# Stick-breaking attention: sums over later key blocks made on VectorE, one product with minus ones per key block

## The chip, the cores and the metric

The kernel runs on one core of one Trainium2 chip. The core has a matrix engine (TensorE, PE in the rows below), a vector engine (VectorE, DVE), a scalar engine (ScalarE, ACT), GpSimd (POOL) and SyncE (SP); GpSimd and SyncE do little here but issue DMAs. The metric is the device time of one execution in microseconds (us), as the median of several.

## The reference, cut to what matters

One layer of an encoder: 512 prompt frames and 32 sample frames go through one input projection, a retention branch of 4 heads, a stick-breaking branch of 8 heads, gates, an output projection and an MLP. The change is in the stick-breaking branch of the prompt.

```python
def stick_breaking_block(q, k, v, q_pos, k_pos):
    z = jnp.einsum('bqhd,bkhd->bhqk', q, k).astype(jnp.float32) * (SB_HEAD_DIM ** -0.5)
    mask = (k_pos[None, :] < q_pos[:, None])[None, None]
    u = jnp.where(mask, jax.nn.log_sigmoid(-z), 0.0)
    after = lax.cumsum(u, axis=3, reverse=True) - u
    w = jnp.where(mask, jnp.exp(jax.nn.log_sigmoid(z) + after), 0.0)
    return jnp.einsum('bhqk,bkhd->bqhd', w.astype(v.dtype), v)
```

For each query the weight of a key needs the sum of `u` over all later keys. The 512 keys are four blocks of 128, and a key block b meets the queries of blocks b to 3.

## The kernel before, in words

All activations lie transposed: 128 features on the partitions, 544 frames (512 + 32) along the free axis, worked on in two halves of 272. A product of fp32 precision is made of three fp32r products of a high and a low part (`exact`, `products`); the parts come from `split` (line 270: ScalarE copies the high part, VectorE subtracts to get the low one). The projection (`gemm`, line 304) is a long row of such 272-column products into banks named `mm`; its weights arrive by DMA (`load_w`), are split and kept two tiles deep.

The heads run as chains, Python generators that stop at each `yield need(...)`. A planner (`Flow`, line 77) keeps an account of free buffers and of a planned clock for TensorE, VectorE and ScalarE. TensorE's order is fixed by it (`manual_schedule` for PE): between the products of a `gemm` it polls the chains and puts in the part of any chain that is ready by the plan; where a buffer is not free, `wait` and `advance` run the chains one after the other until it is. The orders of the other engines come from the scheduler of the tile framework. TensorE then executes its list strictly in this order, whatever the real times.

A chain of a stick-breaking head (`sb_chain`, line 666), for heads 0 to 7, goes like this.

- Scores: `by_blocks` writes z into three PSUM banks (`GROUPS`, `BANKS`): block 0 against 512 queries in the first, block 1 against 384 and block 3 against 128 in the second, block 2 against 256 in the third. In the trace this begins with `at<-qk_hi,qk_hi 128x512`. It makes 1280 columns in all (`PACKED`).
- ScalarE makes |z|, exp and ln over 1280 columns into the tile `e`; VectorE adds max(z, 0). So `e` is -u.
- `packed_parts` (line 658): VectorE copies `e` into `sh` (the high part) and subtracts into `sl` (the low part). There is one pair of `sh` and `sl` for all chains, the planner's `sh=1`; a retention chain needs it too.
- Sums over later keys, on TensorE (lines 688 to 704): each block b gets a product with the triangle `tri` of its own block of `e`, and one product with minus ones (`neg1`) per later block. Blocks 0 to 2 take two fp32r products each, on `sh` and on `sl`; block 3 takes one fp32 product on `e`, which shows as two passes. In the trace: `at<-sh,tri_r`, `at<-sl,neg_r`, `at<-e,neg`, `at<-e,cst`.
- exp of the result, again `packed_parts`, the product with the values (`values_of`, in the trace `at<-sh,vt_hi`), and a copy out.

A retention chain (`retention_chain`, line 799) makes its score tile `pt` in one of the two `e` buffers, splits it with the same `packed_parts` (`sh<-pt`), multiplies by its values (`at<-sh,rv_hi`) and normalizes. `state_chain` (line 889) splits transposed keys into `kt` and multiplies them. `qk_chain` (line 499) normalizes a query or key: sums over partitions (`at<-tmp_r,ones_r`), the reciprocal root (`rstd`), then `qk_hi` and `qk_lo`. The main loop (line 938) starts two stick-breaking heads, then one retention head, four times; before the rotated keys of the next retention head it waits at line 957 for the buffer `rk`, which comes free when the three chains of the last retention head have called `leave` (line 793).

Apart from this `ones` and `neg1` are constant tiles with rounded copies `ones_r` and `neg1_r` (lines 328 to 331 and 622 to 630); `tmp()` is a ring of ten tiles of 544 columns.

Of the kernel before, what the change touches and what calls it, by code (L numbers as in the profile page):

```python
# [9 lines left out]
F32 = mybir.dt.float32  # L10
F32R = mybir.dt.float32r
BF16 = mybir.dt.bfloat16
AF = mybir.ActivationFunctionType
ALU = mybir.AluOpType
# [14 lines left out]
P = 128  # L29

PIECES = {0: (0, 0, 512), 1: (1, 0, 384), 3: (1, 384, 128), 2: (2, 0, 256)}
BANKS = ((0, 512), (512, 512), (1024, 256))
PACKED = 1280
# [162 lines left out]
def need(*events, **parts):  # L196
    return events, parts
# [32 lines left out]
def trunk(ctx: ExitStack, tc: tile.TileContext, a: dict, g32):  # L230
    nc = tc.nc
    flow = Flow(mm=3, at=5, tmp=10, e=2, sh=1, qk0=1, qk1=1, qk2=1, qk3=1, vt=2, rv=1, rk=1, rq=1)
    V, S, T = (Timed(e, n, flow) for e, n in ((nc.vector, "V"), (nc.scalar, "S"), (nc.tensor, "T")))

    ctx.enter_context(tc.manual_schedule(engines={mybir.EngineType.PE}))
    const = ctx.enter_context(tc.tile_pool(name="const", bufs=1))
# [5 lines left out]
    def tmp():  # L242
        return tp.tile([P, NT], F32, tag="tmp", name="tmp")
# [26 lines left out]
    def split(src, hi, lo):  # L270
        S.copy(hi, src)
        V.tensor_tensor(lo, src, hi.bitcast(F32), op=ALU.subtract)
# [52 lines left out]
    wv = const.tile([P, 4, KD], F32, tag="wv", name="wv")  # L325
    nc.sync.dma_start(out=wv, in_=a["vecs"].rearrange("p (n k) -> p n k", k=KD))
    nw = const.tile([P, 4, KD], F32, tag="nw", name="nw")
    ones = const.tile([P, P], F32, tag="ones", name="ones")
    nc.vector.memset(ones, 1.0)
    ones_r = const.tile([P, P], F32R, tag="ones_r", name="ones_r")  # L330
    nc.vector.tensor_copy(ones_r, ones)
    ident = cst[:, C_ID:C_MP]
    epsb = const.tile([P, 1], F32, tag="epsb", name="epsb")
    nc.vector.memset(epsb, EPS)
# [52 lines left out]
    c2 = at.enter_context(tc.tile_pool(name="c2", bufs=1))  # L387
# [129 lines left out]
    with tc.tile_pool(name="xin", bufs=1, side="right") as xp:  # L517
# [3 lines left out]
        for k in range(KD):  # L521
            t = xp.tile([P, NT], F32, tag=f"x{k}", name=f"x{k}")
            nc.sync.dma_start(out=t, in_=a["x"][k])
            xs.append(t)
            w = wv[:, 0, k : k + 1]
# [93 lines left out]


    tri_r = c2.tile([P, P], F32R, tag="tri_r", name="tri_r")
    neg1 = c2.tile([P, P], F32, tag="neg1", name="neg1")
    neg1_r = c2.tile([P, P], F32R, tag="neg1_r", name="neg1_r")
    id_b = c2.tile([P, P], BF16, tag="id_b", name="id_b")
    mp_b = c2.tile([P, P], BF16, tag="mp_b", name="mp_b")
# [2 lines left out]
    nc.vector.memset(neg1, -1.0)  # L628
    nc.vector.tensor_copy(tri_r, tri)
    nc.vector.tensor_copy(neg1_r, neg1)  # L630
    nc.vector.tensor_copy(id_b, ident)
    nc.vector.tensor_copy(mp_b, cst[:, C_MP:C_MS])
    nc.vector.tensor_copy(ms_b, cst[:, C_MS:C_QD])
# [22 lines left out]
                )  # L656

    def packed_parts(x):
        hi = bigp.tile([P, PACKED], F32R, tag="sh", name="sh")
        lo = bigp.tile([P, PACKED], F32R, tag="sl", name="sl")  # L660
        V.tensor_copy(hi, x)
        V.tensor_tensor(lo, x, hi.bitcast(F32), op=ALU.subtract)
        return hi, lo


    def sb_chain(h, vt):
        yield need(("qk", h, 0), ("qk", h, 1), at=3, e=1)
        q_r, k_r = heads.pop((h, 0)), heads.pop((h, 1))
        z = [bank() for i in range(3)]
        e = bigp.tile([P, PACKED], F32, tag="e", name="e", bufs=2)  # L670
        for bi, blocks in enumerate(GROUPS):
            for n, b in enumerate(blocks):
                _, c0, w = PIECES[b]
                by_blocks(z[bi][:, c0 : c0 + w], b, k_r, q_r, n == 0, False)
                T.matmul(z[bi][:, c0 : c0 + P], id_b, mp_b, start=False, stop=True, **SG)
        flow.give(qk0=1, qk1=1)
        for bi, (o, w) in enumerate(BANKS):
            S.activation(e[:, o : o + w], z[bi][:, :w], AF.Abs)
        S.activation(e, e, AF.Exp, scale=-1.0)
        S.activation(e, e, AF.Ln, bias=1.0)  # L680
        for bi, (o, w) in enumerate(BANKS):
            V.scalar_tensor_tensor(
                e[:, o : o + w], z[bi][:, :w], 0.0, e[:, o : o + w], op0=ALU.max, op1=ALU.add
            )
        yield need(sh=1)
        parts = packed_parts(e)
        yield need()
        for bi, blocks in enumerate(GROUPS):
            for b in blocks:
                _, c0, w = PIECES[b]  # L690
                for b2 in range(b, 4):
                    bb, cc, w2 = PIECES[b2]
                    o2 = BANKS[bb][0] + cc
                    out = z[bi][:, c0 + (b2 - b) * P : c0 + w]
                    if b2 == 3:
                        T.matmul(
                            out, tri if b == b2 else neg1, e[:, o2 : o2 + w2], start=False, stop=True, **SG
                        )
                    else:
                        for s in parts:  # L700
                            T.matmul(
                                out, tri_r if b == b2 else neg1_r, s[:, o2 : o2 + w2],
                                start=False, stop=False, **SG,
                            )
        flow.give(sh=1)
        for bi, (o, w) in enumerate(BANKS):
            S.activation(e[:, o : o + w], z[bi][:, :w], AF.Exp)
        flow.give(at=3)
        yield need(("v", h), sh=1, at=1)
        parts = packed_parts(e)  # L710
        yield need()
        ob = bank()
        values_of(ob, vt, slice(0, P), parts, e)
        S.copy(s_all[:, h, :SEQ], ob)
        flow.give(at=1, e=1, sh=1, vt=1)
        flow.finish("sb", h)
# [670 lines left out]
```

## Time and profile before

| what | value |
|---|---|
| median of 3 runs | 1010.27 us (1009.81 to 1010.75) |
| the profiled execution, its own time | 1010.44 us |
| its span | 1008.7 us |
| TensorE busy | 994.0 us, 99% of the span |
| VectorE busy | 661.7 us, 66% |
| ScalarE busy | 513.4 us, 51% |
| 16 DMA engines, moved | 102.73 MB, 102 GB/s on the mean |

The span is the time from the first to the last record of the trace; the profiled execution took 1.74 us more than it. Matmuls overlap in the records: each shows some 290 ns for 272 columns, but the next one starts about 126 ns later. So prices on TensorE are taken here from start to start, and a wait shows as a gap between starts that is larger than that. The attention chains lie between 75 and 460 us of the span; behind them only gates, output projection and MLP follow.

### The profile page before, as it was taken

What the parts mean: (1) busy time and instruction counts of PE and PEld (TensorE: products, weight loads), DVE (VectorE), ACT (ScalarE), POOL (GpSimd) and SP (SyncE); (2) the same over time, 40 slices, a digit from 0 to 9 for tenths busy, and PEclk for the clock granted to TensorE, in tenths of its full rate; (3) what the DMA queues carried; (4) which work ended last, traced back from release to release, by engine and by line L of the source; (5) the groups of instructions that cost most, each with busy time, mean ns of one, the idle gap of its engine ahead of it and who ended that gap; (6) DMA issues with size and microseconds to landing.
All of it is one profiled execution on the core that took longest, in us unless ns stands there. A gap on an engine that the chain in (4) does not pass through costs nothing.

```text
span 1008.7 us, 18661 instructions
## 1 busy us (share of the span) xinstructions
PE 994.0 (99%) x7778; PEld 971.8 (96%) x7778; DVE 661.7 (66%) x1096; ACT 513.4 (51%) x923; POOL 45.7 (5%) x80
## 2 busy tenths in 40 slices
PE   7999999999999999999999999999999999999998
PEld 6999999989999999999999999999999999999998
DVE  7878657755676567646444447976576666666785
ACT  6466656537643675454333335775464445444440
POOL 0000001101000102000000011000000000000000
PEclk9999999999999999999999999999999999999999
DMA  7132213422322135114322336232223333333412
GB/s 247 68 129 94 97 53 94 148 64 99 104 64 74 57 118 165 63 43 137 115 84 85 95 129 194 96 126 84 84 84 104 98 101 97 104 102 112 129 43 89
DMA packets 30933, 102.73 MB, mean 102 GB/s; under 512 B 4096, under 2 KB 6144, under 8 KB 30848
## 3 DMA queue, kind: packets, MB, share of 16 engines
q1 hardware_dynamic: 24768, 80.88, 24.6%
q0 software_dynamic: 6080, 20.65, 6.2%
q8 instruction: 61, 1.00, 0.4%
q14 instruction: 24, 0.20, 0.1%
HBM read 90.51 MB, written 11.01 MB: 101 GB/s over the span
## 4 chain that ended last, share of the span: by engine, by line
PE 96%; ACT 1%; DVE 1%; DMA 0%; issue 0%; SPq 0%; DVEq 0%; ACTq 0%
PE mm L223 70%; PE at L223 26%; ACT tmp L223 1%; DVE tmp L223 1%; DMA x<-in_x 0%; DVE r_all L223 0%; ACT kt L223 0%; DVE tmp_r L223 0%; ACT L223 0%; DVE kt L223 0%; ACT whi L223 0%; SPq L284 0%; DVE x_lo L223 0%; ACT x_hi L223 0%; ACT qk_hi L223 0%
## 5 line engine op out<-in xcount | busy, mean ns | idle before, releaser
L223 PE MATMUL mm<-h_hi,whi 128*128 128x272 f32 x1040 | 305.1, 293 | 0.0
L223 PE MATMUL mm<-h_hi,wlo 128*128 128x272 f32 x1040 | 300.9, 289 | 0.0
L223 PE MATMUL mm<-h_lo,whi 128*128 128x272 f32 x1040 | 300.1, 289 | 0.0
L223 DVE TENSOR_TENSOR wlo<-raw,whi 128x1024 fp32r<-128x1024 f32 (+1 forms) x146 | 167.5, 1149 | 136.9 <-ACT whi L223 136.9
L223 ACT CAST whi<-raw 128x1024 fp32r<-128x1024 f32 (+1 forms) x146 | 144.9, 993 | 191.0 <-PE mm L223 170.0
L223 PEld LDWEIGHTS mm<-h_hi,whi 128*128 128x128 f32 x1040 | 196.6, 189 | 1.9 <-issue 0.6
L223 PEld LDWEIGHTS mm<-h_lo,whi 128*128 128x128 f32 x1040 | 196.8, 189 | 0.2
L223 PEld LDWEIGHTS mm<-h_hi,wlo 128*128 128x128 f32 x1040 | 196.1, 189 | 0.2 <-DVE wlo L223 0.2
L223 PE MATMUL mm<-u_hi,wlo 128*128 128x272 f32 x512 | 148.0, 289 | 0.0
L223 PE MATMUL mm<-u_lo,whi 128*128 128x272 f32 x512 | 147.4, 288 | 0.0
L223 PE MATMUL mm<-u_hi,whi 128*128 128x272 f32 x512 | 147.3, 288 | 0.0
L223 PEld LDWEIGHTS mm<-u_lo,whi 128*128 128x128 f32 x512 | 96.5, 188 | 0.0
L223 PEld LDWEIGHTS mm<-u_hi,whi 128*128 128x128 f32 x512 | 96.4, 188 | 0.0
L223 PEld LDWEIGHTS mm<-u_hi,wlo 128*128 128x128 f32 x512 | 96.2, 188 | 0.0
L223 PE MATMUL at<-f_hi,wlo 128*128 128x272 f32 x320 | 92.5, 289 | 0.0
L223 PE MATMUL at<-f_lo,whi 128*128 128x272 f32 x320 | 92.3, 288 | 0.0
L223 PE MATMUL at<-f_hi,whi 128*128 128x272 f32 x320 | 92.3, 288 | 0.0
L223 ACT ACTIVATE tmp<-tmp 128x272 f32<-128x272 f32 (+2 forms) x148 | 74.7, 547 | 26.8 <-DVE tmp L223 26.4
L223 PEld LDWEIGHTS at<-f_hi,wlo 128*128 128x128 f32 x320 | 60.4, 189 | 0.0
L223 PEld LDWEIGHTS at<-f_hi,whi 128*128 128x128 f32 x320 | 60.3, 189 | 0.0
L223 PEld LDWEIGHTS at<-f_lo,whi 128*128 128x128 f32 x320 | 60.3, 188 | 0.0
L223 ACT ACTIVATE tmp<-mm 128x272 f32<-128x272 f32 x78 | 31.2, 400 | 41.1 <-PE mm L223 41.1
(233 smaller groups left out, 1815.1 us busy)
## 6 DMA issues: line engine op xcount, KB each, us to landing
raw<-in_w SPq DMA_DIRECT2D x142, 512.0 KB, 3.5
x<-in_x SPq DMA_DIRECT2D x8, 272.0 KB, 5.5
o_v<-tmp POOLq DMA_DIRECT2D x8, 272.0 KB, 2.5
o_k<-tmp POOLq DMA_DIRECT2D x8, 272.0 KB, 2.5
x<-in_x POOLq DMA_DIRECT2D x8, 272.0 KB, 4.1
o_y<-x POOLq DMA_DIRECT2D x8, 272.0 KB, 2.4
tmp<-o_y POOLq DMA_DIRECT2D x8, 272.0 KB, 3.9
o_y<-y SPq DMA_DIRECT2D x16, 136.0 KB, 1.8
```

The source lines that it names most:

```text
L223: f(out, *args, **kw)
```

## The change

`packed_parts` gets wider tiles (1536 instead of 1280 columns) and a new step, `later_parts`, follows it in the first half of the chain: VectorE adds block 3 of `e` to the last part of block 2, and block 2 (with block 3 in it) to the last two parts of block 1. Three pieces of 128 columns of these sums are split by `split` into columns 896, 1280 and 1408 of `sh` and `sl`, so that the operands of a block lie 384 columns apart (`spaced`). A block then needs one product pair with minus ones, over 384 columns for block 0 and over 256 for block 1; block 2 keeps its fp32 product with block 3. `ones` and `neg1` are no longer kept: they are written to a `tmp` tile, rounded into `ones_r` and `neg1_r`, and read from these.

```diff
@@ -325,10 +325,11 @@
-    ones = const.tile([P, P], F32, tag="ones", name="ones")
+    ones = tmp()[:, :P]
     nc.vector.memset(ones, 1.0)
     ones_r = const.tile([P, P], F32R, tag="ones_r", name="ones_r")
     nc.vector.tensor_copy(ones_r, ones)
+    ones = ones_r.bitcast(F32)
...
-    neg1 = c2.tile([P, P], F32, tag="neg1", name="neg1")
+    neg1 = tmp()[:, :P]
...
     nc.vector.tensor_copy(neg1_r, neg1)
+    neg1 = neg1_r.bitcast(F32)
...
@@ -656,11 +658,24 @@
     def packed_parts(x):
-        hi = bigp.tile([P, PACKED], F32R, tag="sh", name="sh")
-        lo = bigp.tile([P, PACKED], F32R, tag="sl", name="sl")
-        V.tensor_copy(hi, x)
-        V.tensor_tensor(lo, x, hi.bitcast(F32), op=ALU.subtract)
+        hi = bigp.tile([P, PACKED + 2 * P], F32R, tag="sh", name="sh")
+        lo = bigp.tile([P, PACKED + 2 * P], F32R, tag="sl", name="sl")
+        V.tensor_copy(hi[:, :PACKED], x)
+        V.tensor_tensor(lo[:, :PACKED], x, hi[:, :PACKED].bitcast(F32), op=ALU.subtract)
         return hi, lo
+
+    def spaced(t, o, n):
+        return t.rearrange("p (n c) -> p n c", c=384)[:, o // 384 : o // 384 + n, o % 384 : o % 384 + P]
+
+    def later_parts(e, parts):
+        V.tensor_tensor(e[:, 1152:1280], e[:, 1152:1280], e[:, 896:1024], op=ALU.add)
+        V.tensor_tensor(e[:, 640:896], e[:, 640:896], e[:, 1024:1280], op=ALU.add)
+        for dst, src in ((896, 640), (1280, 768), (1408, 1152)):
+            split(e[:, src : src + P], *[t[:, dst : dst + P] for t in parts])
@@ -684,24 +699,26 @@
         parts = packed_parts(e)
+        later_parts(e, parts)
         yield need()
         for bi, blocks in enumerate(GROUPS):
             for b in blocks:
...
+                bb, c0, w = PIECES[b]
+                o = BANKS[bb][0] + c0
+                own, later = z[bi][:, c0 : c0 + w], z[bi][:, c0 + P : c0 + w]
+                if b == 3:
+                    T.matmul(own, tri, e[:, o : o + w], start=False, stop=True, **SG)
+                    continue
+                for s in parts:
+                    T.matmul(own, tri_r, s[:, o : o + w], start=False, stop=False, **SG)
+                if b == 2:
+                    T.matmul(later, neg1, e[:, 896:1024], start=False, stop=True, **SG)
+                    continue
+                for i, s in enumerate(parts):
+                    T.matmul(
+                        later.rearrange("p (n c) -> p n c", c=P), neg1_r, spaced(s, (512, 1024)[b], 3 - b),
+                        start=False, stop=i == 1, **SG,
+                    )
```

The chain's lengths and buffer times enter the planner's account, so TensorE's list is written in another order, above all where the third and fourth stick-breaking heads (2 and 3) meet the first retention head (0). Three places show it. In the names, `at` is a PSUM bank of a chain, `mm` one of the projection, `neg_r` is `neg1_r` and a number behind a name tells two tiles of one name apart; what stands in brackets is what the instruction waits for.

TensorE before, at the sums over later keys of head 2: the last products of the projection, then the triangle.

```order
L223 MATMUL mm<-h_hi,whi 128x272
L223 MATMUL mm<-h_lo,whi 128x272
L223 MATMUL mm<-h_hi,wlo 128x272
L223 MATMUL at<-sh,tri_r 128x512
L223 MATMUL at<-sl,tri_r 128x512 [waits DVE_49]
L223 MATMUL at<-sh,neg_r 128x384
L223 MATMUL at<-sl,neg_r 128x384
L223 MATMUL at<-sh,neg_r 128x256
L223 MATMUL at<-sl,neg_r 128x256
L223 MATMUL at<-e,neg_736 128x128
```

TensorE now, at the same place: the products of `state_chain` of retention head 0 stand directly ahead of the triangle.

```order
L223 MATMUL at<-rvs_hi,kt_1953 128x256 [waits Activation_49]
L223 MATMUL at<-rvs_lo,kt_1953 128x256
L223 MATMUL at<-rvs_hi,kt_1954 128x256 [waits DVE_49]
L223 MATMUL at<-rvs_hi,kt_1953 128x256
L223 MATMUL at<-rvs_lo,kt_1953 128x256
L223 MATMUL at<-rvs_hi,kt_1954 128x256
L223 MATMUL at<-sh,tri_r 128x512 [waits DVE_49]
L223 MATMUL at<-sl,tri_r 128x512 [waits DVE_49]
L223 MATMUL at<-sh,neg_r 128x384 [waits Activation_49]
L223 MATMUL at<-sl,neg_r 128x384 [waits DVE_49]
L223 MATMUL at<-sh,tri_r 128x384
L223 MATMUL at<-sl,tri_r 128x384
```

From the start of head 2's scores to its triangle there were 78 products of 272 columns on the list before and there are 24 now (beside 18 of 256 columns and two transposes of `state_chain`); the pair with minus ones now waits for ScalarE and VectorE once more.

VectorE before, where the `e` of head 2 is split.

```order
L223 CAST sh<-e 128x1280 [waits DVE_49]
L223 SCALAR_TENSOR_TENSOR tmp<-tmp 128x512 [waits DVE_49]
L223 TENSOR_TENSOR wlo<-raw,whi 128x1024 [waits DMAHW6_49,PE_49,Activation_49]
L223 SCALAR_TENSOR_TENSOR r_all<-tmp,nw 128x512 [waits DVE_49]
L223 SCALAR_TENSOR_TENSOR r_all<-tmp,nw 128x512
L223 TENSOR_TENSOR sl<-e,sh 128x1280
```

VectorE now, the same step of head 2.

```order
L223 TENSOR_TENSOR wlo<-raw,whi 128x1024 [waits DMAHW7_49,PE_49,Activation_49]
L223 TENSOR_TENSOR kt_1954<-at,kt_1953 32x256 [waits Activation_49]
L223 CAST sh<-e 128x1280 [waits DVE_49]
L223 SCALAR_TENSOR_TENSOR sc<-sc,at 128x512 [waits DMASW2_49,PE_49]
L223 TENSOR_TENSOR sl<-e,sh 128x1280 [waits DVE_49]
L223 TENSOR_TENSOR e<-e 128x128 [waits DVE_49]
L223 TENSOR_TENSOR e<-e 128x256 [waits DVE_49]
L223 TENSOR_TENSOR sl<-e,sh 128x128 [waits Activation_49] x3
L223 CAST sh<-pt 128x1280 [waits DVE_49,PE_49]
L223 TENSOR_TENSOR sl<-pt,sh 128x1280 [waits DVE_49,PE_49]
```

The split of the first retention head's `pt` now comes behind head 2's; before it came ahead of it. The split of `kt` and the update of `sc`, which waits for TensorE, have moved in ahead of `sl`.

TensorE before, where the values of the first retention head are multiplied.

```order
L223 MATMUL at<-cst,tmp 32x128 [waits PE_49]
L223 MATMUL at<-cst,tmp 32x128
L223 MATMUL mm<-h_hi,whi 128x272
L223 MATMUL mm<-h_lo,whi 128x272
L223 MATMUL mm<-h_hi,wlo 128x272
L223 MATMUL at<-sh,rv_hi 128x512
L223 MATMUL at<-sl,rv_hi 128x512
L223 MATMUL at<-sh,rv_lo 128x512
```

TensorE now, the same products, some products behind head 2's triangle.

```order
L223 MATMUL at<-tmp_r,ones_r 128x272 [waits PE_49]
L223 MATMUL at<-tmp_r,ones_r 128x272
L223 MATMUL at<-cst,tmp 128x128 [waits Activation_49]
L223 MATMUL at<-cst,tmp 128x128 x3
L223 MATMUL at<-cst,tmp 32x128 [waits Activation_49]
L223 MATMUL at<-sh,rv_hi 128x512 [waits DVE_49,PE_49,Activation_49]
L223 MATMUL at<-sl,rv_hi 128x512 [waits DVE_49]
L223 MATMUL at<-sh,rv_lo 128x512
```

Between head 2's triangle and these there are now the partition sums of a `qk_chain` and the transposes of a value chain, and behind them follow the scores of head 3, with no product of the projection among them: from the two transposes ahead of `kt` to the partition sums of the retention chain the list has no row with `mm`.

## Rows read from the trace of the kernel before

**Rows 1.** The page, part 1: busy us, share of the span, instructions

```profile
PE 994.0 (99%) x7778; PEld 971.8 (96%) x7778; DVE 661.7 (66%) x1096; ACT 513.4 (51%) x923; POOL 45.7 (5%) x80
```

**Rows 2.** Waits of PE: engine, tile, releaser, us in total, times, longest

```profile
PE mm L223 <- ACT whi L223: 5.7, 1, 5.7
...
PE at L223 <- ACT kt L223: 1.1, 1, 1.1
PE at L223 <- DVE so L223: 0.7, 1, 0.7
...
PE at L223 <- ACT tmp L223: 0.5, 1, 0.5
```

**Rows 3.** Timeline of PE at head 0's sums: start, duration, instruction

```profile
94.27 0.28 PE L223 MATMUL at<-sl,neg_r 128*128 128x256 f32 x1
94.39 0.38 PE L223 MATMUL at<-e,neg 128*128 128x128 f32 x2
94.53 0.42 PE L223 MATMUL at<-sh,tri_r 128*128 128x384 f32 x1
94.79 0.34 PE L223 MATMUL at<-sl,tri_r 128*128 128x384 f32 x1
94.97 0.28 PE L223 MATMUL at<-sh,neg_r 128*128 128x256 f32 x1
```

**Rows 4.** Chain of waits in order of time: start, length, a row of 159 products

```profile
40.59 19.98 PE mm L223 x159
```

**Rows 5.** Timelines of PE and DVE: scores and split of heads 1, 2

```profile
101.77 0.40 PE L223 MATMUL at<-qk_hi,qk_hi 128*128 128x512 f32 x1
...
110.94 1.49 DVE L223 TENSOR_TENSOR sl<-e,sh 128x1280 fp32r<-128x1280 f32 x1
...
149.00 0.39 PE L223 MATMUL at<-qk_hi,qk_hi 128*128 128x512 f32 x1
151.19 0.71 PE L223 MATMUL at<-tmp_r,ones_r 128*128 128x512 f32 x2
...
160.82 1.48 DVE L223 TENSOR_TENSOR sl<-e,sh 128x1280 fp32r<-128x1280 f32 x1
...
162.99 0.40 PE L223 MATMUL at<-sh,tri_r 128*128 128x512 f32 x1
```

**Rows 6.** Groups by line and form: count, busy us, mean ns, idle before

```profile
L223 DVE SCALAR_TENSOR_TENSOR r_all<-tmp,nw 128x512 f32<-128x512 f32 x8 | 5.6, 746 | 0.1
L223 DVE TENSOR_TENSOR q<-q,tmp 128x272 f32<-128x272 f32 x8 | 3.5, 433 | 0.0
L223 DVE TENSOR_TENSOR pt<-at,dm 128x128 f32<-128x128 f32 x4 | 1.1, 280 | 0.0
L223 ACT COPY vt<-at 128x128 f32<-128x128 f32 x8 | 2.1, 263 | 5.8 <-DVE vt_lo L223 5.8
```

**Rows 7.** Timelines of DVE and PE: a split of pt, then two qk chains

```profile
132.24 0.83 DVE L223 CAST sh<-pt 128x1280 fp32r<-128x1280 f32 x1 [0.46 <-PE at L223]
133.58 1.49 DVE L223 TENSOR_TENSOR sl<-pt,sh 128x1280 fp32r<-128x1280 f32 x1
...
88.71 0.66 PE L223 MATMUL at<-tmp_r,ones_r 128*128 128x272 f32 x4
96.95 0.68 DVE L223 TENSOR_TENSOR qk_lo<-tmp,qk_hi 128x512 fp32r<-128x512 f32 x1
...
249.10 0.66 PE L223 MATMUL at<-tmp_r,ones_r 128*128 128x272 f32 x4
254.98 0.69 DVE L223 TENSOR_TENSOR qk_lo<-tmp,qk_hi 128x512 fp32r<-128x512 f32 x1 [0.34 <-ACT qk_hi L223]
```

**Rows 8.** Timeline of PE in the opening; clock by windows: length, PE busy, PEclk

```profile
9.67 0.43 PE L223 MATMUL mm<-x_hi,whi 128*128 128x272 f32 x1
9.90 0.43 PE L223 MATMUL mm<-x_lo,whi 128*128 128x272 f32 x1
...
10.00:12.00 2.00, 2.00 (x11) 1.00 1.03 403
```

More of the change, by code (lines that the diff above doesn't have):

```diff
@@ L689, in sb_chain @@
             for b in blocks:
[L690 to L704, printed above, removed]
+                bb, c0, w = PIECES[b]
[14 more added lines that the diff above has]
+                    )
         flow.give(sh=1)
```

## The prediction

> **What bounds the kernel now.** I read the busy times first: TensorE is busy for 994.0 of 1008.7 us, VectorE for 661.7 [rows 1]. So a product that goes away shortens the kernel by its own length, as long as TensorE then finds the next one ready. The waits of TensorE say how well it is fed: all together are about 10 us, of which 5.7 are the first weights in the opening and only 2.3 lie in the attention [rows 2]. There is no slack to win back, and what the change can spoil is the feeding. That it is fed comes from a planner: it lays products of the projection between the steps of a chain, so that VectorE and ScalarE work under them. I therefore look at two things: what leaves TensorE, and how many products the new list still has under each step that it waits for.
>
> **The removed products.** Per head two fp32r pairs with minus ones become one pair for block 0 (256 columns on `sh` and `sl` fall away), and the fp32 products with block 3 of blocks 0 and 1 fall away. A 256-column product takes 0.12 us from start to start (94.27 to 94.39). The fp32 product and the 384-column triangle behind it take 0.40 (94.39 to 94.79), the next one of 384 columns alone 0.18, so the fp32 product costs 0.22 [rows 3]. That is 2 x 0.12 + 2 x 0.22 = 0.68 us a head and **5.4 us** for eight, all on the engine that sets the end.
>
> The pairs that stay read their operand in pieces 384 columns apart. No row of before shows such a read. Its bound from below is the same price as in one piece; from above, each piece of 128 costs what a pass of an fp32 product costs (0.11), so 0.15 more for 384 columns and 0.10 more for 256, 16 of each: 4.1 us. I take nothing, since a piece holds as many columns as such a pass and columns alone set the step from 0.12 to 0.18.
>
> **The added work.** Per head VectorE gets sums over 128 and 256 columns and three subtractions of 128, ScalarE three copies of 128. A 128-column sum takes 0.28 us, one of 272 takes 0.43, a 128-column copy 0.26 [rows 6]: 1.5 us on VectorE and 0.8 on ScalarE, 12 and 6 us in all, on engines with a third and a half of the span free. Off the path they cost nothing. On the chain they lengthen the way from `sl` to the pair with minus ones by 0.28 + 0.43 + 0.26 + 0.28 = 1.25 us, of which the `sl` triangle covers 0.24. In six heads the new list has 16.5 to 19.8 us of TensorE work between the start of the scores and the triangle, counted with the prices above; the chain from the scores to the end of `sl` took 10.7 us in head 1 (101.77 to 112.43) and 13.3 in head 2 (149.00 to 162.30) [rows 5]. With 1.25 more it still fits. The two small tiles of ones and minus ones cost nothing: their copies are 0.2 us each on VectorE, away from any step that TensorE waits for.
>
> **The moved work.** This is the term that decides. In heads 2 and 3 the cover is gone; I go through the list from the start of head 2's scores.
>
> - Head 2. The scores take 2.2 us (149.00 to 151.19) [rows 5]. Up to and with the `sh` triangle there are then 18 products of 256 columns (2.2 us), 24 of the projection at 0.126 each (3.0; 159 took 19.98 [rows 4]), two transposes (0.2) and the triangle (0.24): 7.8 us of work, where it was 14.0 before (149.00 to 162.99). The chain needs 10.7 to 13.3. I take 12.4, nearer the long row, because a weight split, the `kt` split and the `sc` update stand ahead of `sl` on VectorE. TensorE waits 4.6 us there (2.9 to 5.5), then 1.0 to 1.5 for the new sums, which I take as 1.2. Together **5.8** (3.9 to 7.0). Behind the waiting triangle everything else on TensorE queues.
> - The first retention head. The split of its `pt` needs `sh`, which TensorE has only just read. Before, the copy and the subtraction took 2.8 us from start to end (132.24 to 135.07), 2.3 if they stand back to back [rows 7], and a release comes on top. TensorE meanwhile has four products for sums (0.5), five transposes (at most 0.6) and one product of values (0.24). Wait: **1.2** (1.0 to 1.7).
> - The query of head 3. From the sums over partitions to the end of `qk_lo` it took 6.6 us (249.10 to 255.67) and 8.9 (88.71 to 97.63) [rows 7]. On TensorE stand 0.5 + 0.6 + 3.6 (two groups of value products) + 0.24 and the wait of 1.2 just named, 6.1 us. Two full splits lie ahead of `qk_lo` on VectorE, so the long row is the nearer one. Wait: **2.6** (0.4 to 2.8).
> - Head 3. Scores, sums, values and 57 products of the projection make 11.9 us of cover against a chain of about 12.4; then the two `r_all` products (0.75 each [rows 6]) and two rotations stand among the new sums. Wait: 0.5 + 2.4 = **2.9** (1.0 to 4.6).
> - A smaller one ahead of them: the transpose of `so` waited 0.7 us before [rows 2]; its cover shrinks by 0.4 us, and steps of a reciprocal root now stand within its chain. Add **1.0** (0.4 to 1.8). The wait for `tmp` (0.5 [rows 2]) goes with the old order: **-0.5**.
>
> Sum: 5.8 + 1.2 + 2.6 + 2.9 + 1.0 - 0.5 = 13.0 us of new waits against 5.4 us of removed work, so +7.6. The profiled execution took 1010.44 us, 0.2 above the median of the runs; with +7.6 it is **1018.0 us**. All lower ends together give 1011.2, all upper ends 1022.4.
>
> **The rivals.**
>
> *The cover holds: 1005.0 us, faster.* TensorE stays fed, as it is at 99% now [rows 1], and the full 5.4 us are won. For it: VectorE is free a third of the time, and most waits on the old list came out at nothing. It decides at head 2: the chain to `sl` would have to end within 7.8 us of the scores. Against it: the shortest of these chains took 10.7 us [rows 5], and no product of the projection stands in that stretch to hide the rest. 0.07.
>
> *The waits are half of what I cost: about 1010, no change.* Chains run faster where VectorE has no projection to read out, and waits that I add one after the other overlap. Gain and waits cancel at 5.4 us of waits. 0.06.
>
> *TensorE's clock falls in the stretch: about 1021.* In the opening 272-column products stand 0.23 us apart (9.67 to 9.90), twice the 0.126 of later; that is the spacing of 1.2 GHz, after 5.7 us without any product, though the clock column reads 1.00 [rows 8]. Some 30 products there cost 0.10 more each, 3 us. In the new stretch TensorE works only about a fifth of the 6 to 7 us before head 2's pairs. The wait of 1.1 us in the old attention [rows 2] is the longest that before shows there, so nothing tells whether it would fall. It adds 3 us to the forecast. 0.20.
>
> The Trainium skill, page "TensorE: Matmul & The Clock Gate", section "What's actually happening", says that the clock is halved by default and after idle time, and released by sustained work; by that rule the stretch could run its products at half speed, and the trace of the opening agrees (0.23 against 0.126 us).
>
> *The spaced read is slow.* Up to 4.1 us on top, 1022. 0.05.
>
> **How the numbers follow.** The forecast as costed has 0.62 and is the likeliest: 1018. With the clock and the spaced read, slower has 0.87. A measurement of this kernel can tell about 0.2% from no change, 2 us: faster by more than that 0.07, within it 0.06, slower 0.87. For the range I leave out the two cheap rivals below (0.13) and a little above: from 1011, the sum of the lower ends, to 1024, the upper ends and half of the clock's cost.
>
> **What would show it.** Right: the profile after has 5 to 6 us less work on TensorE; its waits grow from 10 to some 23 us, nearly all within 40 us from the start of head 2's scores, put down to VectorE and ScalarE at `at` tiles (`kt`, `sl`, `qk_lo`); TensorE's busy share dips between about 145 and 190 us. Wrong: no such dip, then the sum of the waits fails. If the dip is there and the time still falls, I have mis-sized the chains. If products in the dip stand 0.23 us apart, the clock fell. If `neg_r` products of 384 columns stand more than 0.18 us apart, the spaced read costs.

## The result and the profile after

The changed kernel takes 1020.06 us (median of 5 runs, 1018.82 to 1020.46) against 1010.27 us for the kernel before (1009.81 to 1010.75), measured beside it: a ratio of 1.0097, 95% interval 1.0085 to 1.0108. So it is slower, 9.8 us, 2.0 above the forecast of 1018.0 and inside the range of 1011 to 1024. The profiled execution took 1020.46 us, its span is 1018.7.

The page's first part and its row of TensorE's clock, then TensorE's waits of the changed kernel (in all, times, longest; the opening's waits are left out), to be laid beside [rows 1] and [rows 2]:

```profile
PE 993.3 (98%) x7730; PEld 969.0 (95%) x7730; DVE 672.1 (66%) x1136; ACT 518.6 (51%) x947; POOL 45.9 (5%) x80
...
PEclk9999998999999999999999999999999999999999
```

```profile
PE at L223 <- ACT sh L223: 2.4, 2, 1.9
PE at L223 <- ACT kt L223: 2.4, 2, 1.3
PE at L223 <- DVE sl L223: 2.0, 2, 1.7
PE at L223 <- DVE so L223: 1.9, 1, 1.9
...
PE at L223 <- DVE qk_lo L223: 1.2, 1, 1.2
PE at L223 <- ACT qk_hi L223: 1.2, 1, 1.2
PE at L223 <- DVE kt L223: 0.8, 2, 0.5
```

TensorE has 48 records fewer, six a head (an fp32 product shows as two). Its busy time hardly falls (994.0 to 993.3), for a reason that comes below. The attention had 2.3 us of waits in [rows 2], 2.6 with one of 0.3 for `kt` that stands behind the mark there; now there are 13.0, with 0.6 for `tmp` and 0.5 for `tmp_r` that are not shown here. In all TensorE's waits grew from 10.3 to 21.3 us. Some 10.6 us of them lie between 129 and 190 us, where the prediction put them. The timeline of TensorE through head 2 (start, duration, instruction; in brackets the idle time in the records and who ended it):

```profile
155.29 0.38 PE L223 MATMUL at<-cst,tmp 128*32 128x128 f32 x2
157.00 0.38 PE L223 MATMUL at<-rvs_hi,kt 32*128 32x256 f32 x1 [1.32 <-ACT kt L223]
...
158.04 0.50 PE L223 MATMUL at<-rvs_hi,kt 32*128 32x256 f32 x2 [0.54 <-DVE kt L223]
...
158.78 0.50 PE L223 MATMUL at<-sh,tri_r 128*128 128x512 f32 x1
160.96 0.79 PE L223 MATMUL at<-sl,tri_r 128*128 128x512 f32 x1 [1.69 <-DVE sl L223]
162.27 0.69 PE L223 MATMUL at<-sh,neg_r 128*128 128x384 f32 x1 [0.52 <-ACT sh L223]
162.76 0.53 PE L223 MATMUL at<-sl,neg_r 128*128 128x384 f32 x1
163.09 0.52 PE L223 MATMUL at<-sh,tri_r 128*128 128x384 f32 x1
...
165.29 1.16 PE L223 MATMUL at<-tmp_r,ones_r 128*128 128x272 f32 x4
166.28 0.71 PE L223 MATMUL at<-cst,tmp 128*128 128x128 f32 x5
```

Two things are to be seen. First the gaps in the starts: 155.29 to 157.00 and 158.78 to 160.96 in place of one unbroken row of projection products. Second, from 162.76 on the products follow each other at twice the old distance: 0.33 us for 384 columns, where [rows 3] show 0.18 (94.79 to 94.97). Windows of the same stretch name the reason; the figure behind POOL's is the granted clock:

```profile
155.00:160.00 5.00, 2.41 (x13) 1.38 (x11) 4.83 (x8) 1.59 (x3) 0.77 (x2) 0.94 0.52 162
160.00:163.00 3.00, 1.52 (x3) 0.97 (x4) 2.37 (x6) 0.80 (x3) 0.69 (x2) 0.50 0.42 172
163.00:166.00 3.00, 3.00 (x14) 3.00 (x14) 0.86 (x2) 0.92 (x2) 0.56 (x1) 0.50 0.30 87
166.00:170.00 4.00, 3.71 (x23) 3.17 (x22) 3.17 (x6) 3.79 (x12) 0.00 (x0) 0.97 0.02 4
```

After 155 to 160 us, in which TensorE was busy 2.41 of 5 us, its clock is at 0.50, that is 1.2 GHz in place of 2.4. It is back just after 166 us, with 4 us of unbroken work behind it (from 162.27 on). The same happens once more behind the wait for `so` at 130 us: 12 products of the projection from 131.98 to 134.81 stand 0.23 apart in place of 0.126.

**Where the 10.0 us between the two profiled executions went.** Read start to start on the two timelines:

| term | us |
|---|---|
| products gone: head 0's block took 2.69 (93.34 to 96.03) and takes 1.99 (95.97 to 97.96), 0.70 x 8 | -5.6 |
| head 2: 4.3 up to the end of `sl`, 1.1 for the sums | +5.4 |
| split of the first retention head's `pt` | +0.5 |
| query of head 3 | +2.9 |
| head 3: nothing up to `sl`, 2.3 for the sums | +2.3 |
| `so`, 2.0 in place of 0.9 | +1.1 |
| clock at 1.2 GHz: 1.5 behind `so`, 1.9 from 162.27 to 166.28 | +3.4 |
| first products behind the waits of head 3, further apart though the granted clock is 1.00 there | +0.3 |
| sum | +10.3 |

The sum is 0.3 above what was measured. Waits of 0.3 to 0.5 us for `tmp` and `tmp_r`, of which one went and two came, are not in it.

### The profile page after: what moved, and what is told of

The parts are those of the page before. It is cut to its first block, busy times and chain, and to the rows that moved or that the text cites. A ratio compares the mean times of both kernels' runs of the same rounds, so it can differ in the third digit from the quotient of the medians.

```text
span 1018.7 us, 18638 instructions
## 1 busy us (share of the span) xinstructions
PE 993.3 (98%) x7730; PEld 969.0 (95%) x7730; DVE 672.1 (66%) x1136; ACT 518.6 (51%) x947; POOL 45.9 (5%) x80
## 4 chain that ended last, share of the span: by engine, by line
PE 93%; DVE 3%; ACT 2%; issue 1%; DMA 1%; SPq 0%; DVEq 0%; ACTq 0%
PE mm L223 69%; PE at L223 24%; ACT tmp L223 1%; DVE tmp L223 1%; DMA x<-in_x 1%; DVE r_all L223 0%; ACT e L223 0%; ACT whi L223 0%; DVE sl L223 0%; DVE e L223 0%; ACT kt L223 0%; DVE sh L223 0%; DVE tmp_r L223 0%; ACT sh L223 0%; ACT L223 0%
```

## The experiments

The theory at this point: the removed products are worth 5.6 us, and the new order of TensorE's list takes them back twice over, in waits and in clock. The rivals: the added sums on VectorE and ScalarE cost the time on any list; or the clock is what costs, and the waits alone would be small.

**The list, apart from the work.** The planner's account can be cut loose from what is issued. Two kernels do that. The first issues the changed kernel's work and charges the planner for the old products alone, which gives the old list:

```diff
 def later_parts(e, parts):
-    V.tensor_tensor(...)          # charged
+    nc.vector.tensor_tensor(...)  # not charged; so also the split
...
-    T.matmul(own, tri_r, ...)
+    nc.tensor.matmul(own, tri_r, ...)   # not charged, so also the others
+    # flow.ran("T", length) once for each product of the kernel before
```

> The changed kernel's work (the few products, the sums of later blocks), but the planner is charged for the old products and not for the sums, so that TensorE's list is word for word that of the kernel before, apart from the products with minus ones. Theory (the new list costs the time): the waits of the new list go, the removed products stay gone. In the trace of after the block of head 0 takes 1.99 us from the first triangle to the product behind it, against 2.69 before: 0.70 a head, 5.6 in all. New waits only for the sums, which end 1.64 us after sl in head 2 of after; the old list has 0.93 + 0.24 of that in head 2 and 0.05 + 0.24 in head 3, 3.1 and more in the others but head 7 (1.4): 0.5 + 1.35. So 1010.3 - 5.6 + 1.9 = 1006.6 us. Rival (the sums on VectorE and ScalarE cost the time, wherever they stand): 1015 or more.

Measured: 1011.91 us (11 runs, 1009.18 to 1013.15), ratio to the kernel before 1.0011 (1.0001 to 1.0021). Eight of the changed kernel's ten us are gone, but the removed products are not won either. The trace says where they went. VectorE in head 2 of this run:

```profile
159.65 1.48 DVE L223 TENSOR_TENSOR sl<-e,sh 128x1280 fp32r<-128x1280 f32 x1
161.05 1.22 DVE L223 TENSOR_TENSOR wlo<-raw,whi 128x1024 fp32r<-128x1024 f32 x1
162.19 0.28 DVE L675 TENSOR_TENSOR e<-e 128x128 f32<-128x128 f32 x1
162.39 0.71 DVE L223 TENSOR_TENSOR tmp_r<-tmp,tmp_r 128x544 fp32r<-128x544 f32 x1
163.02 0.41 DVE L676 TENSOR_TENSOR e<-e 128x256 f32<-128x256 f32 x1
163.36 0.28 DVE L680 TENSOR_TENSOR sl<-e,sh 128x128 fp32r<-128x128 f32 x1
163.56 0.71 DVE L223 TENSOR_TENSOR tmp_r<-tmp,tmp_r 128x544 fp32r<-128x544 f32 x1
164.19 0.48 DVE L680 TENSOR_TENSOR sl<-e,sh 128x128 fp32r<-128x128 f32 x2
```

and TensorE beside it:

```profile
162.07 0.40 PE L715 MATMUL at<-sl,tri_r 128*128 128x512 f32 x1
164.02 0.44 PE L720 MATMUL at<-sh,neg_r 128*128 128x384 f32 x1 [1.56 <-ACT sh L679]
164.73 0.44 PE L720 MATMUL at<-sl,neg_r 128*128 128x384 f32 x1 [0.27 <-DVE sl L680]
```

The sums take their 1.4 us of VectorE, as costed, but a weight split of 1.22 and two other splits of 0.71 stand among them, so that the last piece of `sl` comes some 3.5 us after `sl` itself. I had expected 1.64, from head 2 of the changed kernel, where nothing stood between. The old list has no room for 3.5. Laid beside the trace of before, from one block's end to the next, heads 0, 1 and 5 win their 0.7 each, heads 4, 6 and 7 win 0.3 to 0.4, and heads 2 and 3 lose 1.7 and 1.3: 5.5 of the 5.6 go back. (These two profiled executions are 0.2 us apart. The one of this run took 1010.64 us, 1.3 less than the median of its runs, and that 1.3 is not explained by this count.) (The 2.3 for head 3 in the expectation of a later run, below, is 2.0 by this count.) My number missed by 5 us; that the slowdown comes with the list is borne out.

The second is the counterpart, the old work with the charges of the changed kernel.

```diff
         parts = packed_parts(e)
+        # flow.ran("V", ...) and flow.ran("S", ...) for the sums that aren't made
...
-        T.matmul(out, tri if b == b2 else neg1, ...)
+        nc.tensor.matmul(...)     # charged as the fewer products
```

> The work of the kernel before, but the planner is charged for the fewer products and for the sums as in the changed kernel, so that TensorE's list is that of the changed kernel with all the old products in it. Theory (the new list): the waits of after less those for the sums themselves (1.1 in head 2, 2.1 in head 3), and the old products come back: 1020.1 + 5.6 - 3.2 = 1022.5 us, at the least 1019. Its profile shows the dip between 150 and 175 us. Rival (the added work): nothing is added here, so 1010.3 us.

Measured: 1024.29 us (1023.71 to 1024.70), 1.0136 (1.0121 to 1.0152). Nothing of the change is in this kernel but the order, and it loses 14 us. Its waits have the places and releasers of the changed kernel's:

```profile
PE at L223 <- ACT kt L223: 2.4, 2, 1.3
PE at L223 <- DVE so L223: 1.9, 1, 1.9
PE at L706 <- DVE sl L223: 1.7, 1, 1.7
```

It is 1.8 above what I expected. The old products of head 2 stand in the stretch at half clock: from the `sl` triangle on its block takes 4.72 us there (162.79 to 167.51), where head 0 of the kernel before takes 2.46 at full clock (93.57 to 96.03). Between this kernel and the changed one nothing but the work differs: on this list the fewer products with their sums win 4.2 of the 5.6 us.

**The work, apart from the list.** The first of these kernels with the old products in place of the new ones: the sums are made and split, and nothing reads them.

```diff
         parts = packed_parts(e)
+        later_parts(e, parts)   # not charged; against the kernel before
         yield need()
```

> The kernel before with the sums of later blocks and their splits added, which nothing reads, and with the two small tiles of ones and minus ones as in the changed kernel; products and TensorE's list are those of the kernel before. Theory (added work off the path costs nothing): 1010.3 to 1011.5 us. Rival (the added work is what costs): 1020.1 - 1010.3 + 5.6 = 15.4 us more, 1025.7; anything from 1015 up speaks for it.

Measured: 1010.86 us (11 runs, 1009.00 to 1011.49), 1.0001 (0.9993 to 1.0010). VectorE is busy some 10 us more, and the time is the same. The rival that the added work costs the time wherever it stands falls: on the old list, where nothing waits for it, it costs nothing. Nor do the small tiles of ones and minus ones.

**The clock, apart from the waits.** Here products that nobody reads fill the waits, so that TensorE doesn't idle.

```diff
+    def fill(out, n, start=False):
+        for i in range(n):
+            nc.tensor.matmul(out, neg1_r, h_hi[:, 0, :256], start=..., stop=True, **SG)
...
+                    if h == 2 and b == 0:
+                        fill(z[2][:, 256:512], (14, 7)[i])   # behind the sh and the sl triangle
```

> The changed kernel with 45 extra products of 256 columns, into columns that nothing reads, placed where TensorE waits: 13 ahead of the transposes of so (wait 1.85 us), 11 around the transposes of kt (1.49 and 0.70), 14 and 7 ahead of the two waits for sl and the sums of head 2 (1.95 and 1.08). At 0.12 us each they fit in the waits. Theory (the granted clock falls because TensorE idles, and costs time of its own): in after 13 + 2 products behind so stand 0.227 apart in place of 0.126 (1.5 us), those from 162.27 to 166.28 take 4.0 us in place of 2.0 (2.0), some 0.2 beside: with the clock kept up the time falls by 3.7 to 1016.4 us, and the granted clock of 160 to 170 us goes from 0.69 to 0.9 or more. Rival (the clock falls for another reason, or what it costs lies under the waits anyway): 1019.5 to 1021 us.

Measured: 1021.56 us (1021.14 to 1023.21), no gain. The experiment was spoilt: the fill around the transposes of `kt` wrote the bank that the split of `kt` reads, and so waited 2.3 us for that split and delayed what it was to cover. But the rest of its trace speaks. Behind `so` the products stand 0.126 apart, and the block behind the last fill runs from 164.21 to 165.75 in 1.54 us, where the changed kernel took 3.02 (162.27 to 165.29). With the fill of `kt` in another bank:

```diff
         sb_ = bank()
+        if c == 0:
+            fill(sb_[:, :256], 11, True)
```

> As e7_fill, with one thing mended: there the 11 products around the transposes of kt wrote the bank that the split of kt reads, so that they stood behind that split and delayed the chain by 2.9 us at half speed; here they go into the bank of the products behind them, before those start it anew. 45 extra products of 256 columns into columns that nothing reads. Theory (the fall of the clock costs time of its own): in e7_fill the 13 products ahead of the so transposes took the half-speed spacing behind them away and won 1.3 us, and the block behind the last 7 ran 1.95 us shorter. So 1020.1 - 3.3 = 1016.8 us, with a granted clock near 1.0 from 160 to 170 us. Rival (what the clock costs is given back at the next wait, since VectorE's chain sets the end of the stretch): 1019.5 to 1021 us though the spacing is 0.12.

Measured: 1017.69 us (1017.28 to 1019.23), 1.0078 (1.0065 to 1.0092) of the kernel before and 2.4 less than the changed kernel. Windows of this run:

```profile
160.00:163.00 3.00, 2.99 (x23) 2.68 (x21) 1.43 (x4) 1.47 (x4) 0.73 (x1) 1.00 0.27 76
163.00:166.00 3.00, 2.28 (x15) 1.71 (x12) 2.47 (x5) 2.73 (x9) 0.00 (x0) 1.00 0.03 11
186.00:190.00 4.00, 4.00 (x38) 2.51 (x37) 2.46 (x4) 2.34 (x6) 0.00 (x0) 0.61 0.40 127
```

The clock is at 1.00 where it was 0.50, and that wins 3.1 us up to 166 us. Then 0.6 goes back at the split of `pt`, which has less cover now, and 1.5 at 187 to 190 us, where the clock falls in this run and did not in the changed kernel. So the fills account for 1.1 of the 3.2 us between the two profiled executions. Another 0.6 lies in the opening, and 1.5 lies behind a wait for `kt` late in the attention, where no fill stands: there the clock fell in the changed kernel (first row) and not in this run (second row).

```profile
470.00:475.00 5.00, 5.00 (x30) 5.00 (x30) 1.88 (x3) 0.95 (x2) 0.73 (x1) 0.66 0.88 268
470.00:475.00 5.00, 5.00 (x43) 5.00 (x41) 1.50 (x2) 2.62 (x4) 0.00 (x0) 1.00 0.80 295
```

So the fall of the clock costs time of its own, 3.1 us in the two stretches that the fills cover, and two thirds of that go back later. The 2.4 us between the medians can't be put down to the fills alone. The waits are the larger part of the ten us either way.

**Can the removed products be won?** If the wait for the sums is all that ate the gain on the old list, the triangles of the other blocks can stand under it.

```diff
+        for b in (0, 1, 3, 2):
+            own(b)               # the triangle of block b
+        for b in (0, 1, 2):
+            later(b)             # its products with minus ones
...
-                for s in parts:
-                    nc.tensor.matmul(own, tri_r, ...)
...
```

> The run with the old list and the sums (e1_before_account), with TensorE's products of a head in another sequence: first the triangles of all four blocks, then the products with minus ones, so that 0.82 us of triangles stand between the sl triangle of block 0 and the first product that needs a sum. In that run the waits for the sums, laid beside the trace of before, cost 2.2 us in head 2, 2.3 in head 3, 0.26 and 0.31 in heads 4 and 7, and that gave the removed products back. Theory (the wait for the sums, and nothing else, ate the gain there): 0.82 less in heads 2 and 3, the small two gone, 2.2 in all: 1011.9 - 2.2 = 1009.7, and the waits for sh at the products with minus ones fall from 3.1 to 1.5 or less. Rival (the gain went elsewhere, to the opening or to VectorE's added work): no change, 1011.5 to 1012.5.

Measured: 1006.70 us (1005.84 to 1007.65), 0.9967 (0.9954 to 0.9979): faster than the kernel before by 3.6 us, and by 5.2 than the same work in the old sequence. TensorE in head 2:

```profile
161.58 0.40 PE L713 MATMUL at<-sl,tri_r 128*128 128x512 f32 x1
161.81 0.34 PE L713 MATMUL at<-sh,tri_r 128*128 128x384 f32 x1
...
162.50 0.28 PE L713 MATMUL at<-sl,tri_r 128*128 128x256 f32 x1
163.54 0.44 PE L722 MATMUL at<-sh,neg_r 128*128 128x384 f32 x1 [0.75 <-ACT sh L679]
164.25 0.44 PE L722 MATMUL at<-sl,neg_r 128*128 128x384 f32 x1 [0.27 <-DVE sl L680]
```

The wait is 0.75 in place of 1.56, the eight heads are shorter by 0.7 but for heads 2 and 3. The gain is larger than expected. The two profiled executions in the old and in this sequence are 3.8 us apart: 0.8 each comes from heads 2 and 3, 0.3 to 0.4 each from heads 4, 6 and 7, together 2.7; 1.0 goes back at 416 us, where the transposes of the last value chain now wait 0.8 for ScalarE; 1.5 lies at 461 to 464 us and is a matter of the clock (last section); 0.5 lies in the opening. The other 1.4 of the 5.2 is not in these traces, since the execution in the old sequence was 1.3 below its median. The gain over the kernel before does not hang on the clock: among executions with a mean granted clock of 1.000, four here take 1006.4 us on the mean, 18 of the kernel before 1009.7.

The other way is to leave out the change where it isn't covered: the old products and no sums in heads 2 and 3.

```diff
+        sums = h not in (2, 3)
+        if sums:
+            later_parts(e, parts)
...
+            (later if sums else one_by_one)(b)
```

> The old list as in e6_own_first (triangles first), the few products and the sums in heads 0, 1 and 4 to 7, but the old products and no sums in heads 2 and 3, where VectorE's chain ended last. Theory (the removed products are worth 0.70 us a head wherever the sums are covered): six heads give 4.2 and no head waits more than before: 1010.2 - 4.2 = 1006.0 us. Rival (the gain is given back somewhere else too): 1009 or more.

Measured: 1007.04 us (1005.54 to 1007.62), 0.9967 (0.9956 to 0.9979). Laid beside the trace of before, the six heads bring it to 4.2 us ahead by 411 us, as expected, and no product with minus ones waits. Then 1.0 goes back at once: the transposes of the last value chain, which had cover, now wait 0.8 for ScalarE at 416 us. Another 0.5 goes at 669 us, and the end stands 2.7 ahead. So even there a third of the gain is given back at later steps.

**Other lists.** The changed kernel with one number of the planner changed:

```diff
-    MARGIN = 300
+    MARGIN = 50
```

> The changed kernel with one number changed: the planner's MARGIN, 50 in place of 300 (how long a chain's step must have been ready before it is put on TensorE's list). All work and all charges are those of the changed kernel, but the list comes out without the crowding: 99 products of the projection between the scores and the first triangle of head 2 (24 in the changed kernel, 78 before) and 87 in head 3 (57, 72). Theory (the list costs the time, not the sums nor that they are charged): the dip at 150 to 190 us goes and the removed 5.6 us are won, less a little for steps that now come 0.25 us nearer to what they wait for: 1005 to 1008.5, 1007.0 us. Rival (the sums cost on any list where they are charged): 1015 or more.

Measured: 1013.41 us (1013.26 to 1013.99), 1.0034 (1.0021 to 1.0046). Below the rival's 1015, and 5 above the theory's range: neither was right as put. Heads 2 and 3 wait nowhere in this run. But the list that uncrowds them uncovers others:

```profile
PE at L223 <- ACT tmp L223: 6.5, 7, 4.6
```

```profile
198.48 0.29 PE L223 MATMUL mm<-h_hi,wlo 128*128 128x272 f32 x1
203.35 0.97 PE L223 MATMUL at<-cst,tmp 128*128 128x128 f32 x4 [4.59 <-ACT tmp L223]
```

At 198 us the transposes of the sample chain stand 4.6 us too early, `so` waits 1.8 as in the changed kernel, and both waits are followed by half clock.

Which charge turns the list? With the sums charged and the products charged as before:

> The changed kernel, with the planner charged for the sums as in it, but for the old products in place of the fewer ones. This gives a third list: 60 products of the projection between the scores and the first triangle of head 2 (24 in the changed kernel, 78 before), none from there to the scores of head 3, 54 in head 3. Theory (charging the sums is what crowds the chains behind head 2 together): head 2 itself has 12.1 us of work against the 12.3 that its chain took in after, so 0.2 and 1.3 for the sums; the values of head 2 wait for Exp and a split, 3.5 against 1.6 us of work, 2.0; the split of pt 0.9; head 3 with 9.5 against 12.3, 2.8, and 1.5 for the sums: 8.7 against 5.6 won, and 1 us for the clock: 1010.3 + 4.1 = 1014.4 us, 1012 to 1018. Rival (it is the fewer products charged that crowd it): 1005 to 1010 us.

Measured: 1022.49 us (1022.07 to 1024.48), 1.0124 (1.0110 to 1.0138), well outside my 1012 to 1018. The rival falls; charging the sums alone makes a list as bad as the changed kernel's. (The fewer products charged without the sums were not run.) My sum for it missed by 8. The largest wait in it is one that I took for 0.9:

```profile
164.43 0.38 PE L223 MATMUL at<-e,vt 128*128 128x128 f32 x2
168.38 0.79 PE L223 MATMUL at<-sh,rv_hi 128*128 128x512 f32 x1 [3.57 <-DVE sh L223]
```

```profile
160.00:170.00 10.00, 4.14 (x19) 2.88 (x18) 9.89 (x20) 6.15 (x17) 1.13 (x2) 0.84 0.13 45
```

VectorE works 9.89 of these 10 us: the steps of the two reciprocal roots and their queries stand ahead of the split of `pt`. I had counted the split and its release alone. TensorE is busy 4.14, and the clock falls.

Last, the sequence that won on the old list, put on the changed kernel's own:

> The changed kernel with its own list and charges, and only the sequence within a head's block changed as in e6_own_first: all triangles first, the products with minus ones behind them. Theory (there the chain up to sl and the crowding behind it hold TensorE, the sums only for the two waits of 1.08 and 2.08 us in heads 2 and 3): 0.82 less in each, 1020.1 - 1.6 = 1018.5 us. Rival (the sums are what holds TensorE in the changed kernel, as in e1_before_account, where the same sequence won 5.2 us): 1015 or less.

Measured: 1018.90 us (1017.87 to 1020.35), 1.0084 (1.0070 to 1.0097), 1.2 less than the changed kernel, where the theory had 1.6. The intervals of the two kernels overlap, so the 1.2 alone shows little, but the rival's 1015 is out. The waits for `kt`, `so`, `sl` and the query stay (2.4, 1.9, 1.7, 2.4 us); only that for `sh` falls, from 2.4 to 0.4. (Its profiled execution took 1020.35 us, since in that one the clock fell at 173 to 178 us as well.)

## Why the prediction came out

**Removed products: right.** 0.68 a head was forecast, 0.70 measured; 5.4 and 5.6.

**The spaced read: nothing, as taken.** In the changed kernel's head 0 the pairs stand as close as reads in one piece:

```profile
96.43 0.34 PE L223 MATMUL at<-sh,neg_r 128*128 128x384 f32 x1
96.60 0.34 PE L223 MATMUL at<-sl,neg_r 128*128 128x384 f32 x1
96.78 0.34 PE L223 MATMUL at<-sh,tri_r 128*128 128x384 f32 x1
```

0.17 us from start to start, spaced or not (and 0.12 for the pairs of 256 columns behind them). That rival is out.

**Added work off the path: right for six heads, too short for the old list.** It costs nothing as such (1010.86). But its 1.25 us of chain length is only nearly so short (1.64) where VectorE goes straight from `sl` to the sums. The prediction read the order of VectorE in head 2 of the changed kernel and took it for all but head 3; in the run with the old list, with other work between, it is 3.5. (Of the six heads the last has 15.2 us of cover, not the 16.5 that were the least counted; it waits nowhere all the same.)

**Head 2: right.** The chain was taken as 12.4 us and took 12.3 (148.57 to 160.91); the wait 4.6 was 4.3, the sums' 1.2 were 1.1. **`so`: right**, 1.0 and 1.1. **Query of head 3: right**, 2.6 and 2.9.

**The split of `pt`: too high**, 1.2 against 0.5. It began as soon as TensorE had read `sh`, as the prediction said, and the four products and five transposes that were to cover it took 1.46 us instead of 1.1, because the products among them ran at half clock. **Head 3: right in size, 2.9 against 2.3, by another split.** I gave 0.5 to the chain up to `sl` and 2.4 to the sums; the first came to nothing, and the sums took 2.3, with the two `r_all` products of 1.41 us and the rotations between, as foreseen. **The wait for `tmp`: wrong.** I took 0.5 off, since its place went with the old order; a wait of 0.5 for `tmp_r` came elsewhere.

So 12.2 us of waits where 13.0 had been forecast, and 5.6 against 5.4 removed: by these steps alone the time would have been 1017. **What the forecast left to a rival happened: the clock fell.** It was priced at 3 us, in one stretch, with a chance of 0.20; it cost 3.4, in two. The sign given for it, products 0.23 us apart in the dip, is there, and the measured 1020.06 lies nearer to that rival's 1021 than to the forecast's 1018.0. That the forecast missed by 2.1 us and not by 3 is luck: the waits came out 0.8 smaller than costed. The range held without the half of the clock's price that was put on top, since 1020.06 lies below 1022.4, the sum of the upper ends.

The step that failed is a reading. The prediction said that nothing in the trace tells whether a wait of 1.1 us in the attention would let the clock fall. The trace of before has that wait, between the starts at 456.70 and 458.08, for `kt`, with one of 0.3 two products on, and tells: windows just behind it, of the kernel before,

```profile
458.00:462.00 4.00, 3.62 (x21) 3.29 (x22) 3.81 (x6) 1.26 (x3) 0.95 (x2) 0.86 0.59 156
462.00:466.00 4.00, 4.00 (x26) 4.00 (x25) 0.68 (x2) 1.45 (x2) 0.49 (x1) 0.72 0.93 312
```

show the clock at 0.86 and 0.72, and the products 0.23 apart from 460.92 to 464.09. The prediction took the clock from the opening alone [rows 8] and did not read what stands behind the longest wait of the attention. Read so, a fall behind waits of 1 to 2 us was a likely case and not one of 0.20, with a price: 15 products at 0.10 us more each. It was not a certain one: a wait of 1.27 us in the same trace, in the opening at 30.57 us, has a clock of 1.00 around it (28 to 32 us) and products 0.12 to 0.13 apart behind it, and the last section has more of this.

One sign that the prediction gave, 5 to 6 us less work on TensorE, can't be read off its busy time: that fell by 0.7 us where 5.6 us of work left, since a record at half clock is longer (0.43 in place of 0.29 us for 272 columns) and a product that stands alone counts with its full length.

## What to carry to other kernels

Where one engine is 99% busy and a planner writes its list, a removed product is worth its length only on a list that stays fed: price the new list first, and test it by giving the old work the new charges and the new work the old ones, which parts order from work in two runs. Work added to a chain costs what stands between its steps on their engine too, not only the sum of its lengths (3.5 us in place of 1.25 here); reordering the waiting engine's own products (here all triangles first) covered half of the wait, and on the old list won 3.6 us where the old sequence had won nothing. Before a wait is priced, look at the granted clock behind the longest waits that the trace already has.

## What the hardware showed that I had not expected

**The same wait is followed by half clock in one execution and not in the next.** Eleven of the twelve profiled kernels here have the same step late in the attention: a wait of 1.1 us for `kt` and, two products on, one of 0.3. In seven of them (the kernel before and the changed one among them) some 15 products a little later stand 0.23 apart, about 1.5 us; in four none does. The kernel with the sums that nobody reads, over the same stretch as the two rows above:

```profile
458.00:462.00 4.00, 3.71 (x26) 3.37 (x27) 3.81 (x6) 1.18 (x2) 1.02 (x2) 1.00 0.54 168
462.00:466.00 4.00, 4.00 (x34) 4.00 (x34) 1.24 (x2) 2.16 (x3) 0.40 (x1) 1.00 0.92 284
```

Its list and waits there are those of the kernel before, to 0.1 us. It is so with another wait: 1.9 us for the sums of head 3 are followed by half clock in the last run with fills (the row at 186 to 190 us above, 0.61) and not in the changed kernel (1.00 from 186 to 192 us). And the runs of the kernel before show it within one kernel: of 41 executions beside the experiments 18 have a mean granted clock of 1.000 and 20 one of 0.998, and the first take 1009.7 us on the mean, the others 1010.6. So an execution can carry about 1 us (0.9 by these means, 1.5 by the spacing) that another one of the same kernel has not, and two profiles that differ by that much show nothing yet. The Trainium skill, page "TensorE: Matmul & The Clock Gate", section "What's actually happening", says that the hardware watches the activity in a window that runs freely and doesn't start with the kernel; that would let the same wait fall on either side, and the seven and four agree, though no run here shows the window.

**More products made it faster.** 45 products into columns that nobody reads, laid into the waits, kept the clock at 2.4 GHz in both stretches and won 3.1 us there. 2.1 of it went back at later steps, and how much of the 2.4 us between the medians is theirs stays open, since one fall that they don't touch came in one profile and not in the other. Where a wait on a chain can't be removed, that is worth a try, with a bank that nothing in the chain reads: with 11 of the 45 in the wrong bank the kernel took 1021.56 us, no gain.
